# Delta rule's block inverses grown from 16 to 32 as 32x32 products on parts of the array, with a new plan for the order

## The chip, the cores and the metric

One core of a Trainium2 chip runs the program. The metric is the device time of one execution in microseconds (us). The kernel before has a median of 947.4 us over 3 runs (946.87 to 948.32).

## The reference, cut to what matters

Five layers follow each other on a sequence of 256 tokens with 1024 channels: a gated feed-forward layer (f1), a mixer of two attentions (mx), a second feed-forward layer (f2), a block attention (mb) and a gated delta rule (gd). The change bears on the delta rule, which solves a triangular system for each head and each chunk of 64 tokens:

```python
lmat = jnp.einsum('bhncd,bhnjd->bhncj', k_beta, k) * decay_strict
a_mat = lmat + jnp.eye(C, dtype=lmat.dtype)
rhs = jnp.concatenate([v * beta[..., None], k_beta * jnp.exp(g_cum)[..., None]], axis=-1)
sol = lax.linalg.triangular_solve(a_mat, rhs, left_side=True, lower=True, unit_diagonal=True)
```

There are 8 heads. The kernel takes two chunks together as one 128x128 triangle, two triangles a head, and inverts the triangles.

## The kernel before, in words

The whole program is recorded operation by operation, and a planner inside the kernel (`Program.schedule`) then writes the five engines' instruction streams in an order that it works out from ranks, readiness, free buffers and its own prices. So a change of one operation, or of a number in `PLAN`, can move instructions anywhere. Each engine executes its stream in that order. When TensorE's queue has nothing ready, the planner puts in filler matmuls (`bank<-ones 128x128`) whose results nobody reads. All instructions carry the line of one helper, L490, so the trace is read by engine, tile names and shapes. Tiles come from pools: `long` and `half` (fp32 in SBUF), `cut` (the two rounded parts of an fp32 operand, high and low, that ScalarE (ACT) and VectorE (DVE) write one after the other), `bank` (PSUM).

The start (`start`) loads x and c, takes SiLU of c, and builds the first layer's shift and scale from it chunk by chunk: for each of 8 chunks of 128 channels DVE makes weighted sums of the rows of `w_mod` (`long<-long,c_silu`), a one-column matmul turns them into the columns `A_f` and `B_f`, ACT makes the layer's input h from them (`half<-long,B_f,A_f`), and h and the two weight blocks of the chunk (`w_gate`, 1024 wide, and `w_up`, 768 wide) are cut into high and low parts. Then 42 matmuls of the chunk run. `PLAN["ahead"]` says from which chunk on the sums of the next chunk are recorded ahead of this chunk's weights.

The delta rule (`gdn`) has four units u of two heads, so four triangles a unit. `follow` records its steps in the order of `PLAN["gdn"]`: `k` (keys, which fill the triangles Lm), `s` (substitute: the inverses X of all 16x16 diagonal blocks, by DVE, gathered through DRAM into `xc`), `q`, `v`, `z` (projections), `g` (grow, in three parts), `r` (recur: the chain of products that gives the outputs of two heads, ending in a normalisation, a transposition and a cut) and `o` (the output projection, 512-wide matmuls). `grow` before spreads X and its transposed Xt out to block-diagonal 128x128 matrices, makes two rounds of four 128x128 products to get from blocks of 16 to blocks of 32, transposes Xt by TensorE to get X, and only from 32 on works on parts of the array: 32x32 products for 64, and 64x64 products for 128:

```python
for i in range(4):
    mm(ps[:, i, :], lm[:, i, :], Xt[u][:, i, :], start=True, stop=True)
z = self.half(4, P)
V.tensor_tensor(z, ps, self.up16[:, None, :].to_broadcast([P, 4, P]), ALU.mult)
```

Of the kernel before, what the change touches and what calls it, by code (L numbers as in the profile page):

```python
# [15 lines left out]
AF = mybir.ActivationFunctionType  # L16
ALU = mybir.AluOpType
AX = mybir.AxisListType

P = 128  # L20
# [105 lines left out]
class Program:  # L126
# [205 lines left out]
    def schedule(self):  # L332
        ops = self.ops
        for op in ops:
# [150 lines left out]
    def emit(self):  # L485
# [36 lines left out]
    "decay": 0,  # L522
}

# [30 lines left out]
class Net:  # L555
# [406 lines left out]
    def start(self):  # L962


        nc, a = self.nc, self.a
        for t in range(NT):
            nc.sync.dma_start(self.x[t], a["x"][0, t * P : (t + 1) * P, :])
        self.silu("c")
        view = a["w_mod"][0][:, 0 : 2 * D].rearrange("(p k) (s n) -> p k s n", k=KD, s=2)

        def partial(k0, nk):
# [25 lines left out]
        for t in range(NT):  # L997
# [16 lines left out]
        for n, (k0, nk) in enumerate(chunks):  # L1014
# [3 lines left out]
            ps = self.bank()  # L1018
# [12 lines left out]
            for k in range(k0, k0 + nk):  # L1031
# [461 lines left out]
    def gdn_consts(self):  # L1493
        nc = self.nc

        consts = self.half(4, P)
        self.triu, self.tril, self.bd16, self.up16 = (consts[:, i, :] for i in range(4))
# [5 lines left out]
        for m, n, sel in ((self.bd16, 16, (([[-16, 8], [0, 16]], 0, 1), ([[16, 8], [0, 16]], 15, -1))),  # L1503
                          (self.up16, 32, (([[-32, 4], [0, 32]], 0, 1), ([[32, 4], [0, 32]], 15, -1), ([[0, 4], [1, 32]], -16, 0)))):
            nc.gpsimd.tensor_copy(m, self.ones)
            v = m.rearrange("p (b j) -> p b j", j=n)
            for pattern, base, mul in sel:
                nc.gpsimd.affine_select(out=v, in_=v, pattern=pattern, compare_op=ALU.is_ge, fill=0.0, base=base, channel_multiplier=mul)
        self.al, self.dtb = (self.fixed_tile([P, 8], n) for n in ("al", "dtb"))
        for t, n in ((self.al, "gdn_a_log_2"), (self.dtb, "gdn_dt_bias_2")):  # L1510
            v = self.a[n][0]
            nc.sync.dma_start(t, bass.AP(tensor=v.tensor, offset=v.offset, ap=[[0, P], [1, 8]]))
        nc.scalar.activation(self.al, self.al, AF.Exp)
        yield

    def gdn(self, h, after, due):
        nc, a = self.nc, self.a
        V = nc.vector
        w_in = a["gdn_w_in_2"][0]
        tp, mm = nc.tensor.transpose, nc.tensor.matmul  # L1520
# [41 lines left out]
        ps = self.bank()  # L1562
# [16 lines left out]
        for u in range(4):  # L1579
# [6 lines left out]
            ps = self.bank(4, P)  # L1586
# [4 lines left out]
            exps = nc.used(ps)  # L1591
            ps = self.bank(4, P)
# [91 lines left out]
        def grow(u):  # L1684

            xc = blocks[0]
            both = self.long(2, 4, P)
            X, Xt[u] = both[:, 0], both[:, 1]
            lm = Lm[u].rearrange("p h t j -> p (h t) j")
            for n, dst in ((1, Xt[u]), (0, X)):  # L1690
                V.tensor_tensor(dst.rearrange("p i (b j) -> p i b j", b=8), xc[:, n, 4 * u : 4 * u + 4, None, :].to_broadcast([P, 4, 8, 16]),
                                self.bd16.rearrange("p (o b j) -> p o b j", o=1, b=8).to_broadcast([P, 4, 8, 16]), ALU.mult)
            ps = self.bank(4, P)
            for i in range(4):
                mm(ps[:, i, :], lm[:, i, :], Xt[u][:, i, :], start=True, stop=True)
            z = self.half(4, P)
            V.tensor_tensor(z, ps, self.up16[:, None, :].to_broadcast([P, 4, P]), ALU.mult)
            ps = self.bank(4, P)
            for i in range(4):
                mm(ps[:, i, :], X[:, i, :], z[:, i, :], start=True, stop=True)  # L1700
            V.tensor_tensor(Xt[u], Xt[u], ps, ALU.add)
            ps = self.bank(4, P)
            for i in range(4):
                tp(ps[:, i, :], Xt[u][:, i, :], self.ident)
            nc.scalar.activation(X, ps, AF.Copy)
            yield
            q = [slice(32 * j, 32 * j + 32) for j in range(4)]
            ps, z = self.bank(4, P), self.half(4, P)
            for lo, hi in ((0, 1), (2, 3)):
                for i in range(4):  # L1710
                    mm(ps[q[lo], i, 0:32], lm[q[hi], i, q[lo]], Xt[u][q[hi], i, q[hi]], start=True, stop=True)
                nc.scalar.activation(z[q[lo], :, 0:32], ps[q[lo], :, 0:32], AF.Copy)
            ps = self.bank(4, P)
            for lo, hi in ((0, 1), (2, 3)):
                for i in range(4):
                    mm(ps[q[lo], i, 0:32], X[q[lo], i, q[lo]], z[q[lo], i, 0:32], start=True, stop=True)
            for i in range(4):
                mm(ps[q[1], i, 0:32], z[q[0], i, 0:32], X[q[0], i, q[0]], start=True, stop=True)
            for lo, hi in ((0, 1), (2, 3)):
                nc.scalar.activation(Xt[u][q[lo], :, q[hi]], ps[q[lo], :, 0:32], AF.Copy)  # L1720
            nc.scalar.activation(X[q[1], :, q[0]], ps[q[1], :, 0:32], AF.Copy)
            yield
            lo, hi = slice(0, 64), slice(64, P)
            ps, z = self.bank(4, P), self.half(4, P)
            for i in range(4):
                mm(ps[lo, i, 0:64], lm[hi, i, lo], Xt[u][hi, i, hi], start=True, stop=True)
            nc.scalar.activation(z[lo, :, 0:64], ps[lo, :, 0:64], AF.Copy)
            ps = self.bank(4, P)
            for i in range(4):
                mm(ps[lo, i, 0:64], X[lo, i, lo], z[lo, i, 0:64], start=True, stop=True)  # L1730
            nc.scalar.activation(Xt[u][lo, :, hi], ps[lo, :, 0:64], AF.Copy)

        def recur(u, Xt, oT):
            hs = [2 * u, 2 * u + 1]
# [81 lines left out]
        Xt = [None] * 4  # L1816
# [122 lines left out]
```

## Time and profile before

| what | value |
|---|---|
| median of 3 runs | 947.4 us |
| the profiled execution | 948.18 us, its span 946.4 us |
| PE (TensorE) busy | 919.9 us, 97% of the span |
| DVE busy | 765.8 us, 81% |
| ACT busy | 520.4 us, 55% |
| mean granted TensorE clock | 0.992 |

PE stands for TensorE's matmuls, PEld for its weight loads, SP for the queue that issues the transfers. The records of matmuls overlap, each with the latency of one, so a PE that is "busy" throughout need not be fed at its best pace: the number of records in a stretch, and the distance between their starts, say more than the share.

### The profile page before, as it was taken

How to read it: one execution, taken by the hardware profiler on the slowest of the kernel's cores; microseconds unless marked ns; L12 is line 12 of the kernel's file. 1: busy time of each engine (PE TensorE's matmuls, PEld its weight loads, DVE VectorE, ACT ScalarE, POOL GpSimd, SP SyncE). 2: the span in 40 equal slices, each digit the busy share in tenths (PEclk: the TensorE clock that was granted, in tenths of full speed). 3: DMA queues.
4: the chain of work that ended last, by engine and by line, in shares of the span. 5: the costliest groups of instructions: out<-in, count | busy, mean ns of one | idle time of the engine just before them, and what ended most of it. 6: DMA issues, size and time to landing. Idle time of an engine off the chain costs nothing.

```text
span 946.4 us, 17955 instructions
## 1 busy us (share of the span) xinstructions
PE 919.9 (97%) x6925; PEld 855.4 (90%) x6925; DVE 765.8 (81%) x1401; ACT 520.4 (55%) x945; POOL 47.7 (5%) x98
## 2 busy tenths in 40 slices
PE   7999999998999999999999999999999989999996
PEld 7889999998999989988998999989999889999885
DVE  6995589968899989979998764579955699799566
ACT  5474533338862676558444544465565386655560
POOL 7000000002100000001000000000000000200010
PEclk7999999999999999999999999999999999999998
DMA  9997889983352749996999886628955531364101
GB/s 314 348 356 264 300 277 344 353 293 106 112 179 89 251 131 335 347 389 215 341 345 364 317 296 197 191 91 302 385 182 165 171 90 46 101 196 134 47 23 44
DMA packets 153969, 213.66 MB, mean 226 GB/s; under 512 B 14449, under 2 KB 127127, under 8 KB 153884
## 3 DMA queue, kind: packets, MB, share of 16 engines
q1 hardware_dynamic: 153884, 212.52, 66.1%
q8 instruction: 54, 0.88, 0.4%
q14 instruction: 31, 0.25, 0.1%
HBM read 210.11 MB, written 2.36 MB: 225 GB/s over the span
## 4 chain that ended last, share of the span: by engine, by line
PE 82%; DVE 9%; ACT 3%; DMA 3%; issue 2%; SPq 1%; POOL 1%; DVEq 0%; ACTq 0%; POOLq 0%
PE bank L490 82%; DVE half L490 3%; DVE long L490 2%; DVE cut L490 2%; DVE x L490 1%; SPq L490 1%; ACT junk L490 1%; ACT cut L490 1%; DMA long<-in_w_gate_dram 1%; DVE tiny L490 1%; ACT half L490 1%; POOL tiny L490 1%; DMA long<-in_w_up_dram 1%; DMA half<-in_g_pre_ffn_dram 0%; DMA long<-in_gdn_w_in_dram 0%
## 5 line engine op out<-in xcount | busy, mean ns | idle before, releaser
L490 PE MATMUL bank<-cut,cut 128*128 128x256 f32 (+2 forms) x5684 | 793.7, 299 | 4.7 <-DVE cut L490 3.1
L490 PEld LDWEIGHTS bank<-cut,cut 128*128 128x128 f32 x5684 | 735.4, 188 | 44.9 <-DVE cut L490 4.7
L490 DVE TENSOR_TENSOR cut<-long,cut 128x1024 fp32r<-128x1024 f32 (+3 forms) x290 | 341.7, 1194 | 80.5 <-PE bank L490 59.1
L490 ACT ACTIVATE cut<-long 128x1024 fp32r<-128x1024 f32 (+2 forms) x290 | 291.9, 1034 | 139.4 <-PE bank L490 102.6
L490 DVE SCALAR_TENSOR_TENSOR long<-long,c_silu,long 128x1024 f32<-128x1024 f32 (+1 forms) x144 | 142.9, 1013 | 1.0 <-DMA long<-in_w_mod_dram 0.2
L490 ACT ACTIVATE long<-bank 128x512 f32<-128x512 f32 (+9 forms) x148 | 62.6, 448 | 49.1 <-PE bank L490 46.6
L490 POOL TENSOR_TENSOR tiny<-tiny,mhalf 128x1 f32<-128x1 f32 (+1 forms) x32 | 30.9, 965 | 893.2 <-DVE tiny L490 893.2
L490 ACT ACTIVATE half<-bank 128x512 f32<-128x512 f32 (+4 forms) x75 | 35.3, 483 | 39.1 <-PE bank L490 38.8
L490 ACT ACTIVATE cut<-half 128x256 fp32r<-128x256 f32 (+3 forms) x70 | 32.9, 495 | 41.5 <-DVE half L490 41.0
L490 DVE TENSOR_TENSOR cut<-half,cut 128x256 fp32r<-128x256 f32 (+1 forms) x77 | 37.1, 512 | 10.0 <-ACT cut L490 10.0
L490 DVE SCALAR_TENSOR_TENSOR half<-bank,c_cols,half 128x253 f32<-128x253 f32 (+2 forms) x72 | 33.7, 477 | 2.1 <-ACT half L490 1.5
L490 DVE TENSOR_TENSOR half<-bank,long 128x512 f32<-128x512 f32 x20 | 13.7, 690 | 22.5 <-PE bank L490 22.4
L490 ACT ACTIVATE junk<-bank 128x128 bf16<-128x128 f32 (+1 forms) x44 | 16.0, 364 | 25.9 <-DVE half L490 21.7
L490 PE MATMUL bank<-half,long 128*128 128x128 f32 (+3 forms) x240 | 29.4, 258 | 0.0
L490 PE MATMUL bank<-ident,long 128*128 128x128 f32 (+1 forms) x162 | 24.8, 284 | 4.6 <-DVE long L490 3.6
L490 PE MATMUL bank<-long,long 128*128 128x128 f32 (+6 forms) x288 | 28.8, 282 | 0.3 <-ACT long L490 0.3
L490 PE MATMUL bank<-ident,half 128*128 128x128 f32 (+3 forms) x140 | 26.6, 276 | 1.8 <-DMA half<-in_g_pre_ffn_dram 0.9
L490 PEld LDWEIGHTS bank<-long,long 128*64 128x64 f32 (+4 forms) x288 | 20.9, 150 | 6.3 <-issue 1.3
L490 PEld LDWEIGHTS bank<-half,long 128*128 128x128 f32 (+2 forms) x240 | 24.6, 161 | 2.2 <-ACT half L490 0.6
L490 PEld LDWEIGHTS bank<-ident,long 128*128 128x128 f32 (+1 forms) x162 | 19.2, 144 | 6.9 <-DVE long L490 4.9
L490 DVE TENSOR_SCALAR tiny<-tiny 128x1 f32<-128x1 f32 (+3 forms) x67 | 11.6, 172 | 17.1 <-ACT junk L490 15.8
L490 ACT ACTIVATE half<-half,tiny 128x128 f32<-128x128 f32 (+2 forms) x36 | 16.7, 466 | 14.5 <-DVE tiny L490 14.5
(155 smaller groups left out, 509.3 us busy)
## 6 DMA issues: line engine op xcount, KB each, us to landing
long<-in_w_mod_dram SPq DMA_DIRECT2D x56, 512.0 KB, 4.6
long<-in_ada_w_dram SPq DMA_DIRECT2D x48, 512.0 KB, 6.9
long<-in_w_gate_dram SPq DMA_DIRECT2D x44, 512.0 KB, 7.7
long<-in_w_down_dram SPq DMA_DIRECT2D x44, 512.0 KB, 8.9
long<-in_w_up_dram SPq DMA_DIRECT2D x38, 512.0 KB, 7.2
long<-in_w_in_dram SPq DMA_DIRECT2D x38, 512.0 KB, 4.7
long<-in_moba_w_in_dram SPq DMA_DIRECT2D x32, 512.0 KB, 4.6
long<-in_gdn_w_in_dram SPq DMA_DIRECT2D x24, 512.0 KB, 4.0
```

What stands on the lines that cost most here:

```text
L490: getattr(engine, method)(*[real(a) for a in args], **{k: real(v) for k, v in kw.items()})
```

## The change

`grow` no longer spreads the 16x16 blocks out first. It keeps them as 32 columns a triangle (`d`, with X and Xt side by side), and makes the two rounds from 16 to 32 as 32x32 products, four parts of the array in turn: 16 products a unit, then 32, of which 16 give X directly, so that the transposition falls away. After that d is spread out to `Xt[u]` (128 columns) and to half of `X`, off to the side of the next 32x32 products, which read d itself. Two small DVE reductions and three POOL instructions make the masks. In the start, c is loaded and its SiLU taken ahead of x, and `ahead` falls from 9 to 4. `raw` copies the first gate projections of the delta rule and takes their SiLU after the exponentials, `exps` lets the SiLUs of keys and queries go between them. Two steps change places in the mixer, `v0` goes behind the grows, k2 ahead of k1, and two background tasks change places.

```diff
-        self.window, self.counted, self.slow, self.table, self.array = 0.0, 0.0, 2, "exp", (P, P)
+        self.window, self.counted, self.slow, self.table, self.array = 0.0, 0.0, 2, "silu", (P, P)
...
-    "f2": (7, 4, 9, 4, 4, 8, 0, 0, 0, 0, 0),
+    "f2": (8, 3, 9, 4, 4, 8, 0, 0, 0, 0, 0),
     "mixer": (
-        "a v i p . . x0 d2 d1 x1 d0 . s d3 d4 d5 . d6 h0 d7 u5 h1 u0 d8 h2 . h3 . . . e0 . "
-        ". e0 . u3 e1 . u2 e1 . u4 . . u1 . . . u7 z3 z0 . u6 . . z1 . . . . . . z2 ."
+        "a v i p . . x0 d2 d1 x1 d0 . s d3 d4 d5 . d6 h2 h0 d7 . u5 h1 u0 d8 . h3 . . e1 e0 "
+        ". e0 . u3 . u2 . e1 . u4 . . u1 . . . u7 z3 z0 u6 . . . z1 . . . . . z2 . ."
     ),
...
-    "gdn": "k0 k1 k2 k3 s0 q0 q1 g3 g0 q2 q3 g0 z2 g3 g2 z1 g3 g0 v0 g1 g1 g2 g1 r0 v2 v1 r1 g2 o0 r2 . v3 r3",
+    "gdn": "k0 k2 k1 k3 s0 q0 q1 g3 g0 q2 q3 g0 z2 g3 g2 z1 g3 g0 g1 g1 g2 g1 v0 r0 v2 v1 r1 g2 o0 r2 . v3 r3",
...
-    "background": (0, 1, 9, 2, 3, 5, 4, 6, 7, 10, 8),
+    "background": (0, 1, 9, 3, 2, 5, 4, 6, 7, 10, 8),
...
-    "ahead": 9,
+    "ahead": 4,
...
-    "raw": False,
-    "exps": True,
+    "raw": True,
+    "exps": False,
...
+        self.silu("c")
         for t in range(NT):
             nc.sync.dma_start(self.x[t], a["x"][0, t * P : (t + 1) * P, :])
-        self.silu("c")
...
-            both = self.long(2, 4, P)
-            X, Xt[u] = both[:, 0], both[:, 1]
...
+            all = self.long(1024)
+            d, X = all[:, 0:256].rearrange("p (n i j) -> p n i j", n=2, i=4), all[:, 512:768].rearrange("p (i j) -> p i j", i=4)
+            for n in (1, 0):
+                V.tensor_tensor(d[:, n].rearrange("p i (b j) -> p i b j", b=2), xc[:, n, 4 * u : 4 * u + 4, None, :].to_broadcast([P, 4, 2, 16]),
+                                self.bd16.rearrange("p (o b j) -> p o b j", o=1, b=2).to_broadcast([P, 4, 2, 16]), ALU.mult)
+            ps, z = self.bank(4, 32), all[:, 256:384].rearrange("p (i j) -> p i j", i=4)
+            with nc.side_by_side(3):
+                for i in range(4):
+                    for s in q:
+                        mm(ps[s, i, :], lm[s, i, s], d[s, 1, i, :], start=True, stop=True)
+            V.tensor_tensor(z, ps, self.up16[:, None, :].to_broadcast([P, 4, 32]), ALU.mult)
+            ps = self.bank(2, 4, 32)
+            with nc.side_by_side(3):
+                for i in range(4):
+                    for s in q:
+                        mm(ps[s, 1, i, :], d[s, 0, i, :], z[s, i, :], start=True, stop=True)
+                for i in range(4):
+                    for s in q:
+                        mm(ps[s, 0, i, :], z[s, i, :], d[s, 0, i, :], start=True, stop=True)
+            V.tensor_tensor(d, d, ps, ALU.add)
```

On TensorE, the place in the delta rule behind the last 256-wide projection, where the grows begin. Before (the names after the arrow are the moving operand and the weights; `x4` are four products in a row):

```order
4959 L490 MATMUL bank_166<-long_101,long_90 128x128 x4
4960 L490 MATMUL bank_163<-long_96,long_86 128x128 x4
4961 L490 MATMUL bank_165<-long_98,long_91 128x128 x3
4962 L490 MATMUL bank_168<-half_107,long_101 128x128 x4
4963 L490 MATMUL bank_169<-half_108,long_96 128x128 x4
4964 L490 MATMUL bank_165<-long_98,long_91 128x128
4965 L490 MATMUL bank_166<-ident,long_101 128x128 x4
4966 L490 MATMUL bank_163<-long_101,long_90 32x32 x4
4967 L490 MATMUL bank_168<-long_93,long_87 128x128
4968 L490 MATMUL bank_162<-ident,long_96 128x128 x4
```

The same place now:

```order
4961 L490 MATMUL bank_163<-long_100,long_97 32x32 x16
4962 L490 MATMUL bank_168<-long_90,long_103 32x32 x16
4963 L490 MATMUL bank_169<-long_101,long_88 32x32 x16
4964 L490 MATMUL bank_164<-long_93,long_92 32x32 x16
4965 L490 MATMUL bank_168<-ones 128x128
4966 L490 MATMUL bank_169<-ones 128x128
4967 L490 MATMUL bank_164<-ones 128x128 x2
4968 L490 MATMUL bank_163<-long_100 32x32 x32
4969 L490 MATMUL bank_168<-long_90 32x32 x32
4970 L490 MATMUL bank_169<-long_101 32x32 x32
4971 L490 MATMUL bank_164<-long_100,long_97 32x32 x8
4972 L490 MATMUL bank_163<-long_93 32x32 x32
```

The 128x128 products and the transpositions (`ident`) of the grows are gone, 48 products of 32x32 a unit stand in their place, and all four units now begin at once. By the two orders whole, TensorE loses 32 products and 16 transpositions of 128x128, has 272 products of 32x32 instead of 80, 32 of 64x64 as before, and 38 fillers instead of 34.

On ACT, the head of the program, where the SiLU of c is taken. Before:

```order
1 L490 ACT_TABLE_LOAD
2 L490 ACTIVATE junk,tiny_114<-x_171 128x512 x2
3 L490 ACTIVATE junk,tiny_116<-x_172 128x512 x2
4 L490 ACT_TABLE_LOAD
5 L490 ACTIVATE c_silu<-c_raw 128x8
6 L490 ACTIVATE long_95<-bank_162 128x4x128
```

Now:

```order
1 L490 ACT_TABLE_LOAD
2 L490 ACTIVATE c_silu<-c_raw 128x8
3 L490 ACTIVATE junk,tiny_114<-x_171 128x512 x2
4 L490 ACTIVATE junk,tiny_116<-x_172 128x512 x2
5 L490 ACTIVATE long_95<-bank_162 128x4x128
```

The SiLU stands ahead of the squares of x, and one table load is gone.

On DVE, the end of the start: the cuts of the last weights, the last columns `A_f` and the low half of the last chunk of h (`cut<-half`). Before:

```order
86 L490 TENSOR_TENSOR cut_80<-long_91,cut_74 128x1024
87 L490 TENSOR_TENSOR long_93<-long_93 128x256
88 L490 TENSOR_TENSOR cut_79<-long_90,cut_76 128x768
89 L490 SCALAR_TENSOR_TENSOR A_f_179<-bank_167,c_cols 128x1
90 L490 TENSOR_TENSOR B_f_180<-bank_167,c_cols 128x1
91 L490 SCALAR_TENSOR_TENSOR A_f_179<-A_f_179,c_cols 128x1
92 L490 TENSOR_TENSOR cut_84<-long_95,cut_82 128x1024
93 L490 TENSOR_TENSOR cut_63<-long_98,cut_81 128x1024
94 L490 TENSOR_TENSOR cut_85<-long_103,cut_83 128x1024
95 L490 TENSOR_TENSOR cut_77<-half_111,cut_77 128x2x128
```

Now:

```order
85 L490 TENSOR_TENSOR long_90<-long_90 128x256
86 L490 TENSOR_TENSOR cut_76<-long_88,cut_72 128x768
87 L490 SCALAR_TENSOR_TENSOR A_f_179<-bank_167,c_cols 128x1
88 L490 TENSOR_TENSOR B_f_180<-bank_167,c_cols 128x1
89 L490 SCALAR_TENSOR_TENSOR A_f_179<-A_f_179,c_cols 128x1
90 L490 TENSOR_TENSOR cut_80<-long_93,cut_75 128x1024
91 L490 TENSOR_TENSOR cut_79<-long_99,cut_74 128x768
92 L490 TENSOR_TENSOR cut_81<-long_94,cut_82 128x1024
93 L490 TENSOR_TENSOR cut_66<-long_103,cut_85 128x1024
94 L490 TENSOR_REDUCE half_110<-half_112 128x32
95 L490 COPY c_cols<-bank_167 128x77
96 L490 TENSOR_TENSOR cut_73<-half_108,cut_73 128x2x128
```

The last columns are made ahead of the last chunk's two weight cuts instead of behind them, and two other cuts instead of three stand ahead of the low half of h. On ACT the high half of that h now stands behind three cuts, before behind one.

## Rows read from the trace of the kernel before

**Rows 1.** The page, part 1: busy us (share of the span) x instructions.

```profile
PE 919.9 (97%) x6925; PEld 855.4 (90%) x6925; DVE 765.8 (81%) x1401; ACT 520.4 (55%) x945; POOL 47.7 (5%) x98
```

**Rows 2.** Windows: stretch and its length, busy us of each engine (x instructions), clock, DMA.

```profile
core 0: us, PE busy (x) PEld busy (x) DVE busy (x) ACT busy (x) POOL busy (x), PEclk, DMA share, GB/s
...
25.00:63.00 38.00, 34.82 (x280) 33.11 (x278) 37.98 (x92) 21.07 (x30) 0.00 (x0) 1.00 1.05 346
...
218.00:230.00 12.00, 9.54 (x70) 8.49 (x69) 11.03 (x21) 11.54 (x25) 2.69 (x2) 1.00 0.40 122
230.00:430.00 200.00, 199.56 (x1588) 184.93 (x1587) 178.98 (x424) 124.44 (x247) 5.31 (x6) 1.00 0.66 227
...
753.00:771.00 18.00, 14.94 (x101) 13.01 (x100) 17.63 (x36) 10.81 (x22) 1.94 (x2) 1.00 0.20 59
...
857.00:874.20 17.20, 17.20 (x148) 17.06 (x147) 16.11 (x31) 9.79 (x20) 1.01 (x1) 1.00 0.62 172
874.20:907.90 33.70, 33.32 (x397) 29.32 (x396) 19.69 (x42) 19.50 (x58) 1.01 (x1) 1.00 0.15 48
```

**Rows 3.** Timeline of PE from the first grow on: start, duration, engine, operation, records.

```profile
874.24 2.62 PE L490 MATMUL bank<-long,long 128*128 128x128 f32 x22
...
878.71 0.60 PE L490 MATMUL bank<-ident,long 128*128 128x128 f32 x4
879.24 0.85 PE L490 MATMUL bank<-long,long 32*32 32x32 f32 x10
...
887.23 1.14 PE L490 MATMUL bank<-half,long 64*64 64x64 f32 x16
...
907.97 0.94 PE L490 MATMUL bank<-cut,cut 128*128 128x512 f32 x3
908.74 1.72 PE L490 MATMUL bank<-half,long 128*128 128x128 f32 x14
...
923.11 14.82 PE L490 MATMUL bank<-cut,cut 128*128 128x512 f32 x63
```

**Rows 4.** Timeline of PE, 892.9 to 893.7 us: 32x32 products of three kinds.

```profile
893.07 0.34 PE L490 MATMUL bank<-long,long 32*32 32x32 f32 x5
893.22 0.21 PE L490 MATMUL bank<-half,long 32*32 32x32 f32 x1
893.25 0.19 PE L490 MATMUL bank<-long,long 32*32 32x32 f32 x1
...
893.31 0.19 PE L490 MATMUL bank<-half,long 32*32 32x32 f32 x1
893.31 0.19 PE L490 MATMUL bank<-long,long 32*32 32x32 f32 x1
893.31 0.21 PE L490 MATMUL bank<-long,half 32*32 32x32 f32 x1
...
893.43 0.32 PE L490 MATMUL bank<-long,half 32*32 32x32 f32 x5
```

**Rows 5.** Timeline of PE, 882.7 to 884.5 us: 32x32 products into one bank.

```profile
882.75 0.35 PE L490 MATMUL bank<-half,long 32*32 32x32 f32 x7
882.91 0.21 PE L490 MATMUL bank<-long,half 32*32 32x32 f32 x1
...
882.97 0.19 PE L490 MATMUL bank<-long,half 32*32 32x32 f32 x1
882.97 0.19 PE L490 MATMUL bank<-half,long 32*32 32x32 f32 x1
```

**Rows 6.** Timelines of DVE and ACT in the delta rule: a grow's spreading, a recur's first copy.

```profile
863.58 2.49 DVE L490 TENSOR_TENSOR long<-half,half 128x512 f32<-128x512 f32 x4
...
890.34 0.39 ACT L490 ACTIVATE half<-bank 128x256 f32<-128x256 f32 x1 [0.43 <-PE bank L490]
```

**Rows 7.** Timelines of ACT, DVE and PE in the start.

```profile
7.49 1.28 ACT L490 ACT_TABLE_LOAD   x1
...
9.62 1.71 DVE L490 TENSOR_SCALAR long<-long,c_silu 128x256 f32<-128x256 f32 x2
...
59.14 3.50 DVE L490 TENSOR_TENSOR cut<-long,cut 128x1024 fp32r<-128x1024 f32 x3
62.55 0.42 DVE L490 TENSOR_TENSOR cut<-half,cut 128x256 fp32r<-128x256 f32 x1
...
63.02 17.14 PE L490 MATMUL bank<-cut,cut 128*128 128x256 f32 x117 [1.07 <-DVE cut L490]
```

**Rows 8.** Windows of PE alone in the start.

```profile
10.00:12.00 2.00, 1.69 (x8) 0.50 1.06 364
18.00:20.00 2.00, 2.00 (x11) 0.57 1.25 305
```

More of the change, by code (lines that the diff above doesn't have):

```diff
@@ L1496, in gdn_consts @@
         consts = self.half(4, P)
-        self.triu, self.tril, self.bd16, self.up16 = (consts[:, i, :] for i in range(4))
+        self.triu, self.tril, self.bd32 = (consts[:, i, :] for i in range(3))
+        self.bd16, self.up16 = consts[:, 3, 0:32], consts[:, 3, 32:64]
         for m, step, base in ((self.triu, 1, 0), (self.tril, -1, -1)):
@@ L1500, in gdn_consts @@
             nc.gpsimd.affine_select(out=m, in_=m, pattern=[[step, P]], compare_op=ALU.is_ge, fill=0.0, base=base, channel_multiplier=-step)
-        for m, n, sel in ((self.bd16, 16, (([[-16, 8], [0, 16]], 0, 1), ([[16, 8], [0, 16]], 15, -1))),
-                          (self.up16, 32, (([[-32, 4], [0, 32]], 0, 1), ([[32, 4], [0, 32]], 15, -1), ([[0, 4], [1, 32]], -16, 0)))):
+        wide = self.half(2, P)
+        for m, dst, n, sel in ((self.bd32, None, 32, (([[-32, 4], [0, 32]], 0, 1), ([[32, 4], [0, 32]], 31, -1))),
+                               (wide[:, 0], self.bd16, 16, (([[-16, 8], [0, 16]], 0, 1), ([[16, 8], [0, 16]], 15, -1))),
+                               (wide[:, 1], self.up16, 32, (([[-32, 4], [0, 32]], 0, 1), ([[32, 4], [0, 32]], 15, -1), ([[0, 4], [1, 32]], -16, 0)))):
             nc.gpsimd.tensor_copy(m, self.ones)
@@ L1508, in gdn_consts @@
                 nc.gpsimd.affine_select(out=v, in_=v, pattern=pattern, compare_op=ALU.is_ge, fill=0.0, base=base, channel_multiplier=mul)
+            if dst is not None:
+                nc.vector.tensor_reduce(dst, m.rearrange("p (b j) -> p j b", j=32), AX.X, ALU.add)
         self.al, self.dtb = (self.fixed_tile([P, 8], n) for n in ("al", "dtb"))
@@ L1686, in grow @@
             xc = blocks[0]
-            both = self.long(2, 4, P)
-            X, Xt[u] = both[:, 0], both[:, 1]
             lm = Lm[u].rearrange("p h t j -> p (h t) j")
[L1690 to L1704, printed above, removed]
@@ L1705, in grow @@
-            nc.scalar.activation(X, ps, AF.Copy)
+            q = [slice(32 * j, 32 * j + 32) for j in range(4)]
+            lo, hi = slice(0, 64), slice(64, P)
+            all = self.long(1024)
[3 more added lines that the diff above has]
+                                self.bd16.rearrange("p (o b j) -> p o b j", o=1, b=2).to_broadcast([P, 4, 2, 16]), ALU.mult)
@@ new lines, in grow @@
+            V.tensor_tensor(d, d, ps, ALU.add)
+            ps, z = self.bank(4, 32), all[:, 384:512].rearrange("p (i j) -> p i j", i=4)
+            with nc.side_by_side(2):
+                for i in range(4):
+                    for a, b in ((0, 1), (2, 3)):
+                        mm(ps[q[a], i, :], lm[q[b], i, q[a]], d[q[b], 1, i, :], start=True, stop=True)
+            for a in (0, 2):
+                nc.scalar.activation(z[q[a]], ps[q[a]], AF.Copy)
+            Xt[u] = Xts[u]
+            for n, dst, s in ((1, Xt[u], slice(0, P)), (0, X[lo], lo)):
+                m, k = s.stop, dst.shape[2] // 32
+                V.tensor_tensor(dst.rearrange("p i (b j) -> p i b j", j=32), d[s, n, :, None, :].to_broadcast([m, 4, k, 32]),
+                                self.bd32[s, 0 : 32 * k].rearrange("p (o b j) -> p o b j", o=1, j=32).to_broadcast([m, 4, k, 32]), ALU.mult)
@@ L1706, in grow @@
             yield
-            q = [slice(32 * j, 32 * j + 32) for j in range(4)]
-            ps, z = self.bank(4, P), self.half(4, P)
-            for lo, hi in ((0, 1), (2, 3)):
+            ps = self.bank(2, 4, 32)
+            with nc.side_by_side(2):
                 for i in range(4):
-                    mm(ps[q[lo], i, 0:32], lm[q[hi], i, q[lo]], Xt[u][q[hi], i, q[hi]], start=True, stop=True)
-                nc.scalar.activation(z[q[lo], :, 0:32], ps[q[lo], :, 0:32], AF.Copy)
-            ps = self.bank(4, P)
@@ L1714, in grow @@
-            for lo, hi in ((0, 1), (2, 3)):
+                    for a in (0, 2):
+                        mm(ps[q[a], 1, i, :], d[q[a], 0, i, :], z[q[a], i, :], start=True, stop=True)
                 for i in range(4):
[L1716 to L1720, printed above, removed]
@@ L1721, in grow @@
-            nc.scalar.activation(X[q[1], :, q[0]], ps[q[1], :, 0:32], AF.Copy)
-            yield
[L1723 to L1730, printed above, removed]
@@ L1731, in grow @@
-            nc.scalar.activation(Xt[u][lo, :, hi], ps[lo, :, 0:64], AF.Copy)
+                    mm(ps[q[1], 0, i, :], z[q[0], i, :], d[q[0], 0, i, :], start=True, stop=True)
+            for a, b in ((0, 1), (2, 3)):
+                nc.scalar.activation(Xt[u][q[a], :, q[b]], ps[q[a], 1], AF.Copy)
+            nc.scalar.activation(X[q[1], :, q[0]], ps[q[1], 0], AF.Copy)
+            yield
+            ps, z = self.bank(4, 64), all[:, 768:1024].rearrange("p (i j) -> p i j", i=4)
+            with nc.group():
+                for i in range(4):
+                    mm(ps[lo, i, :], lm[hi, i, lo], Xt[u][hi, i, hi], start=True, stop=True)
@@ L1733, in recur @@
+            nc.scalar.activation(z[lo], ps[lo], AF.Copy)
+            ps = self.bank(4, 64)
+            with nc.group():
+                for i in range(4):
+                    mm(ps[lo, i, :], X[lo, i, :], z[lo, i, :], start=True, stop=True)
+            nc.scalar.activation(Xt[u][lo, :, hi], ps[lo], AF.Copy)
         def recur(u, Xt, oT):
@@ L1815, in gdn @@
         steps = dict(k=keys, q=queries, v=values, z=lambda u: u < PLAN["firsts"][2] - 1 or z_proj(u), s=lambda u: substitute(), g=grow, r=lambda u: recur(u, Xt[u], oT), o=output)
-        Xt = [None] * 4
+        Xt, Xts = [None] * 4, self.pairs(4, 4, P)
         going = self.follow("gdn", steps)
```

## The prediction

> **What bounds the kernel now.** I read the page first: TensorE is busy for 97% of the span, DVE for 81% [rows 1]. Records of matmuls overlap with their latency, so I went through windows and compared what a stretch holds (records by the distance of their starts) with its length. In most of the program both agree: of the 200 us from 230 on PE is busy for 199.56 us, and DVE, at 178.98, keeps up [rows 2]. There only less work for PE helps. Three kinds of stretch differ. In the start, DVE is busy for 37.98 of 38 us and the DMA share is 1.05, while PE has 34.82 [rows 2]: DVE and the transfers set the pace together. At three change-overs between layers PE lacks some 3 us each (2.5 and 3.1 in the two that end at 230 and 771), while DVE or ACT is full [rows 2]. The third is the tail, from the first grow on.
>
> The tail is bound by latencies. At 874.24 the last projection is through and the grows begin; at 890.34 ACT makes the first recur's copy, 16.1 us later [rows 3, 6]; the first 512-wide product of the output projection starts at 907.97, 17.6 us behind the copy; the last ends at 923.11 + 14.82 = 937.9 [rows 3]. From the first grow that is 63.7 us. PE looks full in 874.2 to 907.9 (33.32 of 33.7 us), and yet starts only 397 records there, many of them some 20 ns apart, with DVE at 19.69 and ACT at 19.50 [rows 2, 4]. From the counts and distances I get 24.8 us of useful work, 1.3 of fillers and some 7.6 in which PE waits for copies. So fewer rounds, or cheaper ones, before the first recur shorten this stretch; the same inverses do not come out earlier because DVE is fast: the spreading ran at 863.58, 10.7 us ahead of the first grow [rows 6].
>
> **The change, part by part.** *The prices of the products.* A 128x128 product of fp32 has two records: x14 in 1.72 us with the last one's latency of some 0.2 in it is 0.108 us a record, 0.215 a product [rows 3]. Transpositions: the four that start at 878.71 are through when the next starts at 879.24 [rows 3]: 0.11 each. The sixteen 64x64 records in 1.14 us give about 0.06, 0.13 a product [rows 3]. A filler costs as much as a product, 0.21.
>
> The price of the new 32x32 products, four parts of the array in turn, is the open one, since grow before uses at most two parts at once. Alone, one part starts five records from 893.07 to 893.22, 30 ns a record; seven from 882.75 to 882.91, 23 ns [rows 4, 5]. Where products of two units and of two parts mix, thirteen start between 893.22 and 893.43, 16 to 17 ns a record [rows 4]. Bounds: at the top no overlap at all, 23 to 30 ns; at the bottom a quarter of that for four parts, about 7 ns. I take 17, the nearest row to a mixed stream.
>
> The Trainium skill ("TensorE: Matmul & The Clock Gate", Part 3) has tiles of different rows of the array start about 4 ns apart, which would put four of them near the lower bound; by that the tail would gain about 2.5 us more than below.
>
> *The tail now.* By the order, 272 products of 32x32, 16 of the 64x64 ones and 12 fillers stand ahead of the first recur's first product. 272 x 2 x 17 ns = 9.2 us; 16 x 0.13 = 2.1; 12 x 0.21 = 2.6; about ten changes between shapes at 0.09 us (878.71 to 879.24 is 0.53 us, less 4 x 0.11 [rows 3]) = 0.9. Together 14.8 us, and with the last copy of ACT the first recur starts about 15.6 behind the first grow, against 16.1. Recur is untouched; its chain from copy to output keeps 17.6 us: 33.2. Behind the first output stood 96 products of 512 at 0.23 us (x63 in 14.82 [rows 3]) = 22.2, 22 of 128x128 = 4.7 and 12 transpositions = 1.3: 28.2 of the 30.0 us. Now, by the order, 15 of the 128x128 products remain there: 26.7. Of the 1.8 us of waiting I leave 0.5, since twelve 512-wide products now stand right ahead of the last four transpositions, more than the stall of half a microsecond that the copies cause there. 33.2 + 27.2 = 60.4 against 63.7: **-3.3 us**. At 7 ns a record the products cost 5.4 us less, of which I count half, since waits for DVE and ACT then show: -5.8. At 23 to 30 ns it is 0 to +3.8; the break-even lies near 25 ns a record.
>
> *The start.* c's SiLU leads and one table load of 1.28 us goes from ACT's head [rows 7]; the first sums, which need it, start at 9.62 on DVE [rows 7] and may come by that earlier. At the end of the start, three cuts of 3.50 us together stand ahead of the low half of the last h, and PE, which needs it, waits 1.07 us for it and starts at 63.02 [rows 7]; now two cuts stand there, about 1.1 us less. But ACT's high half now stands behind three cuts instead of one, and the transfers, full at 1.05 [rows 2], do not get faster. From 0 (transfers decide) to -2.1; I take **-0.8**.
>
> *Change-overs.* Three fillers fewer by the order, at most 0.2 us each, and order changes where DVE or ACT is full: **-0.4**, from +0.5 to -1.
>
> *At nothing:* the mixer's exchanged steps, f2's pace, the two background tasks and v0 behind the grows stand in PE's full stretches [rows 2], where order moves no end. `raw` and `exps` change ACT's table loads ahead of the grows, DVE's spreads of 256 instead of 512 are shorter, and the masks' extra POOL and DVE work lies far ahead (POOL is at 5% [rows 1]). The cover of all these is the 10.7 us by which the spread blocks wait for PE [rows 6]; without it a table load costs 1.28 us.
>
> Sum: -3.3 - 0.8 - 0.4 = -4.5 us. The profiled execution takes 948.2 us (span 946.4 and 1.8 around it), 0.8 above the median; 947.4 - 4.5 gives **943.0 us**.
>
> **Rivals.** *One part at a time.* The four parts of a round write to one bank of PSUM, and each could wait for the other's write. Then a record costs 23 to 30 ns [rows 4, 5], and with 0 to +3.8 in the tail and -1.2 elsewhere the time is 946 to 950. Against it: two products of different parts have the same start, 882.97 [rows 5], and by the order they write to the same bank. The Trainium skill ("TensorEngine Tiling (Array Packing)", Restrictions and Gotchas) says that different row tiles cannot access the same bank at once; it would give this rival's time, and the row disagrees with it as far as starts tell. 15%.
>
> *Each change of the part costs like a change of shape* (slower). 192 products more, each on another part than the one before, at 0.09 us as between 128x128 and 32x32 [rows 3], are +17 us, and the time about 957. It decides from some 0.025 us a change on. Against it speak the starts 10 to 30 ns apart where parts alternate [rows 4]. 7%.
>
> *The clock.* In the start PE is granted 0.50 at 10 to 12 us and 0.57 at 18 to 20, with 8 and 11 records in 2 us [rows 8]. The tail now has a stretch of some 15 us of small products. If the clock fell there for 9 us, as in the start, half of it would be lost, 4.5 us, which eats the gain: about 947. Against it: before, with 397 records in 33.7 us, it was granted 1.00 [rows 2]. 7%.
>
> *More.* Four parts at 7 ns a record, or the start at its lower bound of -2.1: 937 to 940. 9%.
>
> **How the numbers follow.** The forecast (940 to 945.5) has 62%. Above it lie the serial parts and the clock, at 945.5 to 950 (22%), and the 957; below it the 9%. A range of 938 to 947 leaves out the 957, most of the serial case and the deepest part of the gains, together 2 in 10. What the measurement tells from no change is about 0.2%, 1.9 us: faster ends at 945.5, slower begins at 949.3. Faster: 62 + 9 and 1 of the clock, 72%. The same: the clock's other 6, and 9 of the serial parts, 15%. Slower: 13%, of the serial parts 6 and the costly change of parts 7.
>
> **What will show it.** In the timeline of PE from the first grow on: 32x32 records 17 ns apart (7: more; 25 or above: the serial rival). First grow to the first recur's copy: 15.6 us; copy to the first 512-wide output: 17.6; from there to the last end: 27.2. The granted clock in the tail: 1.00. The start of PE's long stretch at 63.02 comes 0.8 earlier, and the first sums at 9.62 by up to 1.3. I would be wrong if the rounds turn out bound by DVE's and ACT's copies between them, which then show as PE idle with no gain from cheap products, or if the first grow comes late behind the spread.

## The result and the profile after

The changed kernel takes 956.1 us (median of 4 runs, 955.3 to 956.7) against 947.9 in the same runs of the kernel before: 1.0089 times as long, 95% interval 1.0076 to 1.0102. The forecast was 943.0, faster than before; the kernel came out 8.3 us slower. The profiled execution has a span of 954.9 us, 8.5 more than before.

Page of the changed kernel, part 1, to set against [rows 1]:

```profile
PE 926.1 (97%) x7237; PEld 861.1 (90%) x7237; DVE 763.4 (80%) x1411; ACT 517.1 (54%) x944; POOL 47.0 (5%) x101
```

The share of PE says nothing of the loss; the waits of PE do (idle time by releaser: sum, times, longest):

```profile
PE bank L490 <- issue: 4.2, 2, 2.1
```

"issue" is idle time for which the profile shows no releaser; the kernel before has no such row. Windows of the changed kernel, columns as in [rows 2]:

```profile
218.00:230.00 12.00, 9.49 (x70) 8.48 (x69) 11.11 (x21) 11.54 (x25) 2.69 (x2) 1.00 0.36 111
753.00:771.00 18.00, 14.96 (x99) 12.97 (x98) 17.17 (x34) 10.01 (x21) 1.95 (x2) 1.00 0.11 30
874.50:877.90 3.40, 3.40 (x213) 3.04 (x213) 2.78 (x11) 0.78 (x3) 0.00 (x0) 1.00 0.80 242
877.90:880.00 2.10, 0.01 (x2) 0.01 (x2) 1.68 (x4) 0.81 (x1) 0.00 (x0) 1.00 0.08 31
880.00:881.40 1.40, 1.35 (x128) 1.25 (x128) 0.59 (x2) 0.00 (x0) 0.00 (x0) 1.00 0.05 12
881.40:883.40 2.00, 0.00 (x0) 0.00 (x0) 2.00 (x5) 0.00 (x0) 0.00 (x0) 0.60 0.00 0
883.40:890.00 6.60, 6.56 (x167) 5.79 (x168) 4.80 (x11) 3.21 (x12) 0.00 (x0) 0.50 0.02 5
890.00:912.00 22.00, 22.00 (x172) 19.70 (x173) 3.94 (x8) 10.56 (x29) 0.00 (x0) 0.50 0.30 96
912.00:918.00 6.00, 6.00 (x49) 5.73 (x49) 4.37 (x15) 3.92 (x15) 1.01 (x1) 0.96 0.01 3
```

The change-overs lack as much of PE as before. The tail differs: TensorE stands still for 2.1 us, executes 128 matmul records (two to an fp32 product) and 128 weight loads in 1.4 us, stands still for 2 us again, and from then on is granted half its clock until about 912.5. The same place in the timeline of PE:

```profile
874.55 1.44 PE L490 MATMUL bank<-long,long 32*32 32x32 f32 x128
875.94 1.17 PE L490 MATMUL bank<-ones 128*128 128x128 f32 x8
877.04 0.85 PE L490 MATMUL bank<-long 32*32 32x32 f32 x76
879.99 1.17 PE L490 MATMUL bank<-long 32*32 32x32 f32 x114 [2.09 <-issue]
...
883.44 0.26 PE L490 MATMUL bank<-long,long 32*32 32x32 f32 x2 [2.09 <-issue]
```

The first 128 records in 1.44 us, the last one's latency of some 0.2 in it, are 10 ns a record with four parts of the array: nearer the lower bound of 7 than the 17 that I took. Both idle stretches lie within a row of products that one copy had already released, so no round waits there. Between them lie just 256 instructions, 128 records and 128 loads. The DMA view of 880 to 882 has one packet of the queue of instructions:

```profile
q8 instruction: 1, 0.02, 3.2%
```

In windows of 0.2 us such packets stand at 877.6, 881.0 and 884.4, 3.4 us apart, and each stop ends some 2.4 us behind its packet (879.99, 883.44). The pages count 54 such packets in the program before and 57 now, for 2 x 6925 and 2 x 7237 matmul records and loads of TensorE: a packet for every 254 to 256 of them. So TensorE uses a packet's 256 instructions up in 1.4 us here and waits for the next.

The landmarks of the tail: the first recur's copy on ACT, then the first and the last stretch of 512-wide products on PE.

```profile
898.53 0.38 ACT L490 ACTIVATE half<-bank 128x256 f32<-128x256 f32 x1
```

```profile
918.45 1.71 PE L490 MATMUL bank<-cut,cut 128*128 128x512 f32 x6 [0.17 <-ACT cut L490]
...
933.71 12.74 PE L490 MATMUL bank<-cut,cut 128*128 128x512 f32 x54
```

From the first grow at 874.55: 24.0 us to the copy (forecast 15.6), 19.9 to the first output (17.6), 28.0 to the end at 946.45 (27.2); 71.9 in sum, against 63.7 before and 60.4 forecast.

### The profile page after: what moved, and what is told of

Same layout as the page of the kernel before. It is cut to its first block, busy times and chain, and to the rows that moved or that the text cites. A ratio compares the mean times of both kernels' runs of the same rounds, so it can differ in the third digit from the quotient of the medians.

```text
span 954.9 us, 18597 instructions
## 1 busy us (share of the span) xinstructions
PE 926.1 (97%) x7237; PEld 861.1 (90%) x7237; DVE 763.4 (80%) x1411; ACT 517.1 (54%) x944; POOL 47.0 (5%) x101
## 5 line engine op out<-in xcount | busy, mean ns | idle before, releaser
L490 ACT ACTIVATE cut<-long 128x1024 fp32r<-128x1024 f32 (+3 forms) x290 | 292.1, 1034 | 147.8 <-PE bank L490 110.5
L490 ACT ACTIVATE long<-bank 128x512 f32<-128x512 f32 (+9 forms) x156 | 63.7, 432 | 61.0 <-PE bank L490 57.8
L490 POOL TENSOR_TENSOR tiny<-tiny,mhalf 128x1 f32<-128x1 f32 (+1 forms) x32 | 29.3, 915 | 902.5 <-DVE tiny L490 895.6
L490 ACT ACTIVATE half<-bank 128x512 f32<-128x512 f32 (+2 forms) x63 | 32.0, 519 | 36.7 <-PE bank L490 36.5
L490 DVE SCALAR_TENSOR_TENSOR half<-bank,c_cols,half 128x255 f32<-128x255 f32 (+2 forms) x72 | 33.3, 477 | 2.7 <-ACT half L490 2.0
L490 PE MATMUL bank<-long,long 32*32 32x32 f32 (+6 forms) x384 | 28.2, 271 | 2.1 <-issue 2.1
L490 PE MATMUL bank<-long 32*32 32x32 f32 (+5 forms) x512 | 27.1, 244 | 2.5 <-issue 2.1
L490 PEld LDWEIGHTS bank<-long,long 32*32 32x32 f32 (+4 forms) x384 | 21.4, 150 | 7.5 <-issue 3.6
L490 PEld LDWEIGHTS bank<-long 32*32 32x32 f32 (+4 forms) x512 | 22.6, 146 | 4.4 <-issue 2.9
L490 ACT ACTIVATE half<-half,tiny 128x128 f32<-128x128 f32 (+2 forms) x36 | 16.7, 465 | 13.7 <-DVE tiny L490 13.7
L490 DVE TENSOR_SCALAR tiny<-tiny 128x1 f32<-128x1 f32 (+3 forms) x67 | 11.3, 171 | 14.6 <-ACT junk L490 13.1
```

The costliest lines, as they stand in the source:

```text
L490: getattr(engine, method)(*[real(a) for a in args], **{k: real(v) for k, v in kw.items()})
```

## The experiments

There are two theories for the idle stretches, **code** (TensorE runs out of instructions, as above) and **rounds** (it waits for copies between the rounds), and two for the clock, **idle** (it falls because TensorE stands still) against **small** (it falls because small products use little of the array). Times are medians, each beside runs of the kernel before on the same chip (947.4 to 947.6).

**Is it code?** `twice` changes the emission of the changed kernel:

```diff
-            for method, args, kw in op.calls:
+            twice = op.engine == "tensor" and op.parts == (32, 32) and len(op.calls) >= 16
+            for method, args, kw in op.calls * (2 if twice else 1):
```

> The changed kernel with the 32x32 products of grow's first two rounds issued twice (192 products, so 384 weight loads and 384 products more as instructions), the same results. Code: TensorE uses up a 16 KB block of its instructions (256 of them) in 1.4 us there, and blocks come 3.4 us apart; three blocks more give about three more idle stretches of 2 us with no releaser, five in all, and 7 to 11 us more than the changed kernel. Rounds: if the two idle stretches are waits for copies between the rounds, their number stays at two, and the added products cost what such products cost, 20 ns at full clock or 46 at half: 4 to 9 us.

It takes 968.2 us (965.9 to 968.7), 12 more than the changed kernel. The waits of PE:

```profile
PE bank L491 <- issue: 8.9, 5, 2.7
```

Five idle stretches instead of two, three for three blocks more, as code has it and rounds doesn't. The time is a little above code's 7 to 11.

`wide_fill` puts in wide fillers (`small` is an op of 12 or more 32x32 products):

```diff
...
+                if small and i and i % 12 == 0:
+                    bank = args[0].t.slot[:, 256:512]
+                    self.nc.tensor.matmul(bank.rearrange("p (b j) -> p b j", b=2), ones, ones[:, None, :].to_broadcast([P, 2, P]), start=True, stop=True)
```

> The changed kernel with a filler of 256 columns (0.43 us at full clock) behind every 12 of the 32x32 products within a round, into free columns of the same bank; 16 of them, about 6.9 us. Code: the fillers stretch 256 instructions from 1.4 to 3 us and more, blocks arrive in time, the idle stretches of 2.09 us shrink below 0.8 us in sum, the clock stays at 1.00, and the time is 946 to 950 in spite of the work added. Rounds: the idle stretches stay, and the time is the changed kernel's plus up to 7 us, 956 to 963.

It takes 950.4 us over 10 runs (948.9 to 960.5), 1.0047 (1.0021 to 1.0072) times before: less than the changed kernel, with more work. The trace has 12 of these fillers, not the 16 of the expectation; by the starts in the timeline (874.86 to 875.49 for the first) each takes 0.63 us with its changes of shape, 7.6 us in all. In the profiled execution (949.6) no idle time is without releaser, and the clock holds (windows of PE: busy, clock, DMA, GB/s):

```profile
874.00:880.00 6.00, 6.00 (x168) 1.00 0.56 172
880.00:885.00 5.00, 5.00 (x170) 1.00 0.01 3
885.00:890.00 5.00, 5.00 (x173) 1.00 0.01 3
890.00:900.00 10.00, 9.61 (x175) 1.00 0.31 107
```

Two of its runs (956.8 and 960.5) have a mean clock of 0.987 and 0.982, where the others have 0.990 to 0.997; there the clock seems to have fallen after all, but they have no trace. The landmarks of the profiled one:

```profile
897.79 0.38 ACT L495 ACTIVATE half<-bank 128x256 f32<-128x256 f32 x1
```

```profile
911.48 1.70 PE L495 MATMUL bank<-cut,cut 128*128 128x512 f32 x6
...
926.73 12.74 PE L495 MATMUL bank<-cut,cut 128*128 128x512 f32 x54
```

From its first grow at 874.54 these are 23.3, 13.7 and 28.0 us. The order of its own products is that of the changed kernel, and none of the added fillers stands behind 888. So the stretch from the copy to the first output prices the clock: 13.7 us at 1.00, 19.9 in the changed kernel, which has half the clock up to 912.5. That is 6.2 us, more than the 4.2 of the two stops. Less 7.6 of fillers, the 64.9 us of its tail are 57.3, and the stretch ahead of the copy is 15.7, as forecast. This estimate leaves out waits that the fillers may hide. By it the changed kernel's 71.9 us are 14.6 too long, of which 4.2 are the stops and some 10 the clock.

**What lets the clock fall?** `part_fill` narrows the fillers to one part:

```diff
...
-                    bank = args[0].t.slot[:, 256:512]
+                    bank, part = args[0].t.slot[0:32, 256:512], ones[0:32]
```

> As the kernel with wide fillers, but each filler uses one 32x32 part of the array only (256 columns through 32 rows and 32 columns of weights), so that TensorE's time is filled with the same number of instructions and columns while 15 of 16 parts rest. The blocks of code come in time again if the fillers stretch them (idle with no releaser below 1 us in sum). Small: if small products don't keep the clock up, it falls to 0.50 all the same within the grows, and the time is 956 to 963. Idle: if what let the clock fall is that TensorE stood still, it stays at 1.00, and the time is that of the wide fillers, 949 to 951.

It takes 955.5 us (953.7 to 956.4). Idle without releaser is down to 1.4 us in two pieces (0.8 the longest), and still:

```profile
885.00:888.00 3.00, 2.43 (x68) 1.00 0.00 0
888.00:890.00 2.00, 2.00 (x68) 0.84 0.03 8
890.00:900.00 10.00, 10.00 (x97) 0.50 0.34 107
```

The clock falls with a TensorE that stands still for 1.4 us in sum: small products don't keep it up, as "small" has it, though the stops were not quite gone (1 us was the condition) and the time is just below the 956 that "small" gave. `hold` and `hold_long` make TensorE of the kernel before wait where the grows begin:

```diff
...
+            if op in held:
+                bank = op.calls[0][1][0].t.slot
+                self.nc.tensor.matmul(bank[:, :P], ones, ones, start=True, stop=True)
+                for _ in range(3):
+                    self.nc.scalar.activation(self.junk.real(), bank[:, :], AF.Copy)
```

> The kernel before, with TensorE held up twice for about 2.2 us where the grows begin (ahead of the first and the third unit's first round, it waits for three copies of ACT out of a bank), all its own products as they were. Idle: standing still there is what lets the clock fall; it goes to 0.50 within a few us and stays for 10 us or more, and the time is 956 to 962 (4.4 of waiting, 5 to 10 of half clock). Small: if the clock of the changed kernel falls because small products don't keep it up, it stays at 1.00 here, and the time rises by the waits alone, at most 4.4 us: 949 to 952.

> The kernel before with the two holds made longer, seven copies of ACT each instead of three, about 4.2 us each. Idle: if enough standing still lets the clock fall whatever the products are, it goes to 0.50 here, and the time is 960 or more (8.4 of waiting, and 5 to 10 of half clock, less 2 that the tail's other waits take up). Small: it stays at 1.00, and the time is 954 to 957.

`hold` takes 953.6 us (951.9 to 955.0), between its two forecasts. In the profiled execution (952.3) there are two waits of 2.0 us, and the clock stays at 1.00:

```profile
874.00:880.00 6.00, 2.27 (x18) 1.00 0.00 0
```

`hold_long` takes 961.5 us (961.2 to 961.6), as "idle" had it. It has two waits of 4.5 us, and the clock falls towards the end of the first, with products of the whole array alone around it:

```profile
874.00:878.00 4.00, 0.21 (x2) 1.00 0.05 22
878.00:880.00 2.00, 1.33 (x6) 0.51 0.00 0
...
895.00:900.00 5.00, 4.74 (x79) 1.00 0.63 196
```

So neither theory is right alone. Standing still for 4.5 us does it, twice 2.0 us didn't in the execution that was profiled, and small products do it with little standing still. The burst of the changed kernel has both, and which of them its fall needs is not shown.

**Which part of the change?** `old_grow` is the kernel before with the changed plan and start, `new_grow` the kernel before with the new grow alone.

> The changed kernel with grow and its masks as before: the new plan and start alone. If what the change loses lies in the new grow (TensorE stands still for 2.09 us twice there, then 30 us at half clock), this kernel has neither and takes what the first grow's start says, 0.3 us more than before: 947 to 949. If the new plan itself costs the 8 us, it takes 953 or more.

> The kernel before with the new grow and its masks alone; plan, start, raw and exps as before. Grow: if the new grow costs what the change loses, its burst of small products is here too: one or more idle stretches of 2 us with no releaser, a fall of the clock, and 953 to 960. Plan: if the new plan and the grow don't suit each other, it takes 943 to 950.

Both times miss. `old_grow` takes 952.8 us (951.0 to 956.0), between its two forecasts: the new plan with the old grow loses 5.4 us. In its profiled execution, the fastest (951.0), it is level with before at 761.87, and then TensorE waits 1.56 us for DVE ahead of the grows, the first of which starts at 876.01 instead of 874.24. The tail from there is 63.5 us, before's 63.7, and the rest of the program's end takes 1.3 more. Where the other executions lose up to 5 us more is open. `new_grow` takes 960.3 us (951.8 to 961.5), just above its first forecast, with two idle stretches without releaser (2.4 us in all) and half the clock from about 875 to 902.5. One of its four runs, 951.8 with a mean clock of 0.994 against 0.976 to 0.980 of the others, seems to have kept the clock. So the fall comes with the new grow under either plan, if not in every execution; and the two losses, 5.4 and 12.8, don't add up to the 8.3 of both together.

**Can it be mended?** `t_first` gathers the transposed inverses first, `dve_t` lets DVE make X:

```diff
-            for n, src in enumerate((xb, xbt)):
+            for n, src in ((1, xbt), (0, xb)):
```

```diff
...
-                for i in range(4):
-                    for s in q:
-                        mm(ps[s, 0, i, :], z[s, i, :], d[s, 0, i, :], start=True, stop=True)
-            V.tensor_tensor(d, d, ps, ALU.add)
+            V.tensor_tensor(d[:, 1], d[:, 1], ps, ALU.add)
+            V.transpose(d[:, 0], d[:, 1])
```

> The changed kernel with the transposed inverses gathered through DRAM ahead of the plain ones. The first round needs only the transposed ones, and in the trace of the changed kernel they are gathered second and spread at 874.21, just ahead of the first grow. Now 64 of the 272 products run up to 9 us earlier between the projections. Code: the burst then has 256 instructions fewer, so one idle stretch at most of 2.1 us, or none; if the clock stays at 1.00, 944 to 950; if the clock falls all the same, 952 to 956.

> The changed kernel with X at 32 taken from X's transposed by DVE, which transposes 32x32 blocks within themselves (one instruction a unit), instead of by 16 products of TensorE a unit: 64 products, so one block of 256 instructions, less within the grows. Code: one idle stretch of 2 us with no releaser goes; if the clock stays up with it, the time falls to 946 to 949, if the clock falls all the same, to 951 to 955. Rounds: if DVE's copies between the rounds were the limit, a transposition more on DVE makes it slower than the changed kernel, above 956.

`t_first` takes 958.2 us (957.3 to 961.4), `dve_t` 959.3 (954.8 to 960.4). Each has one idle stretch of 2.0 us instead of two, as code has it, but the clock falls in both, at about 879 and 882. One block less is not enough. Both times lie above what code gave (952 to 956 and 951 to 955). That of `dve_t`, above 956, is what rounds gave: from 870 on its trace has 2.2 us of waits for DVE's `long`, which the changed kernel lacks there, 1.4 of them before and in the grows. So a part of its loss is DVE's; only the fastest of its runs has a trace, and what the others lost is open.

The next six tell the planner of the code (`BLOCK` is 3450 ns). They also have a new order of the delta rule's steps and new ranks, found with that rule; all but two of them (`dve_t_told`, `dve_t_fill`) have `ahead` at 5, and `told_b` and `both_c` have `raw` off. No run has the rule without a new order.

```diff
...
+        self.code += sum(2 if m == "transpose" or args[1].dtype == F32R else 4 for m, args, _ in op.calls)
+        if self.code >= 256:
+            self.code -= 256
+            now = self.block = max(now, self.block + self.BLOCK)
```

> The changed kernel with the planner told of the code: in its prices of TensorE a block of 256 instructions can't begin less than 3.45 us after the one before, and for that rule it has a new order of the delta rule's steps (ranks of g and r, ahead 5). The products are the same. Code: the idle stretches without releaser shrink, since other units' rounds and fillers stand between the small products; if the clock then stays at 1.00, 944 to 948. If the small products hold the clock down even so, 952 to 957.

> Both together: X at 32 by DVE's transposition, and an order from the planner that is told of the code. Code: no idle stretch without releaser over 1 us; with the clock at 1.00 it takes 940 to 944 and beats both kernels; with a fall of the clock in the grows 948 to 953.

> As the kernel with both, with a filler of 256 columns behind every 12 products of the first two rounds: 8 of them, 3.4 us of TensorE's time. Small: if the small products let the clock fall in the kernel without them, this one keeps it at 1.00 and is the faster of the two, 942 to 946; if that one keeps its clock, this one is 2 to 3 us slower than it.

The orders of these three leave work out: in `told` one unit's inverses are taken from an unfinished triangle, and in all three unit 2's recur runs without its growth from 64 to 128, whose products still run. `told` takes 951.9 us (948.7 to 958.3), `dve_t_told` 941.5 (940.6 to 945.2), `dve_t_fill` 946.2 (945.6 to 950.8). `told` still has a stop of 2.1 us, and half the clock behind it. In `dve_t_told` the only wait without releaser is 0.3 us, and its clock is 1.00 from 874 to 930; the eight fillers, which it doesn't need, cost 4.7 us instead of 2 to 3. Since work was missing, three more have orders that keep everything; that of `told_b`:

```diff
...
-    "gdn": "k0 k2 k1 k3 s0 q0 q1 g3 g0 q2 q3 g0 z2 g3 g2 z1 g3 g0 g1 g1 g2 g1 v0 r0 v2 v1 r1 g2 o0 r2 . v3 r3",
+    "gdn": "k0 k2 k1 k3 s0 q0 q1 g3 g0 q2 q3 g0 z2 g3 z1 g2 g3 g0 g1 g2 g1 g1 v0 r0 v2 v1 r1 g2 o0 r2 . v3 r3",
```

> The changed kernel, every product of it, with the planner told of the code (no block of 256 instructions of TensorE begins less than 3.45 us after the one before) and an order of the delta rule's steps that suits that rule and keeps every step behind what it reads. Code: one idle stretch of 2 us at most; with the clock at 1.00, 944 to 948; with a fall of the clock 949 to 957. In either case faster than the changed kernel.

> X at 32 by DVE's transposition of 32x32 blocks, and a planner told of the code, with an order that keeps every step behind what it reads. If a burst of fewer small products, with other work between its parts, is supplied with code and keeps the clock, no idle stretch without releaser is over 1 us, the clock is 1.00 in the tail, and the time is 940 to 945, faster than the kernel before. If the shorter time of the kernel that had this first came from the growth that it left out, 946 or more.

> As both_b, another order of the same steps (with the first gates' SiLU taken early, raw off). The same: 940 to 945 if code and clock are the cause; 946 or more if one lucky order was. If it has an idle stretch of 2 us or a fall of the clock and both_b has none, the one with them is 3 us or more slower.

`told_b` takes 945.7 us (945.1 to 947.2 in 10 runs), 0.9983 (0.9974 to 0.9992) times before, with the changed kernel's own products. `both_c` takes 943.6 us (942.3 to 950.0), 0.9964 (0.9949 to 0.9980), the fastest complete one by its median. `both_b` takes 945.8 us, 0.9977 (0.9954 to 1.0000), above its forecast of 940 to 945, but in two groups: five runs at 941.0 to 943.7 with a mean clock of 0.993 to 0.997, five at 947.8 to 948.8 with 0.985 to 0.989. The profiled executions of both have no idle time without releaser in the tail and a clock of 1.00 from 874 to 915. That of `both_b` is of its first group; that the clock falls in the others is read from the mean alone.

In the timeline of `told_b` fillers and a transposition stand between rounds of two units, and no idle stretch is without releaser:

```profile
875.52 0.75 PE L497 MATMUL bank<-long,long 32*32 32x32 f32 x64 [1.58 <-DVE long L497]
876.20 1.51 PE L497 MATMUL bank<-ones 128*128 128x128 f32 x8
877.64 1.93 PE L497 MATMUL bank<-long 32*32 32x32 f32 x128
879.50 1.86 PE L497 MATMUL bank<-ones 128*128 128x128 f32 x10
881.29 0.69 PE L497 MATMUL bank<-long,long 32*32 32x32 f32 x32
```

Even here the clock falls, behind the wait for DVE and with small products, but it is back within some 4 us (busy, clock, DMA, GB/s):

```profile
876.00:878.00 2.00, 2.00 (x66) 0.73 0.83 307
878.00:880.00 2.00, 2.00 (x122) 0.50 0.08 27
880.00:882.00 2.00, 2.00 (x43) 0.91 0.03 8
```

Its first recur's copy comes 17.0 us after the first grow (892.52), the first output 13.9 later (906.37), and the end at 935.5, 29.1 behind that: 60.0 us for the tail, where the forecast said 60.4.

## Why the prediction was wrong

- **The step that failed** is the price of the products ahead of the first recur, "272 x 2 x 17 ns = 9.2 us", as all that the burst costs. The pace of a product was better than that, 10 ns a record. But the sum has no term for the code: at a block of 256 instructions every 3.4 us and four instructions a product, a long burst comes to some 53 ns a product (an estimate from the packets). In the trace this is 4.2 us of standing still.
- **The clock** was a rival with 7% and a price of 4.5 us for 9 us at half clock. It came, and stayed for some 30 us (about 882 to 912.5); why so long is not shown. From the copy to the first output alone it cost 6.2 us against `wide_fill`, more than the two stops together, and by the estimate there some 10 us in the whole tail. "Against it: before, with 397 records in 33.7 us, it was granted 1.00" was a bad reason: 224 of the 397 were products on parts, but the other 173, of the whole array at 0.108 us, stood between them and took 18.7 us. In `part_fill` 32x32 products, with fillers on one part between them, did not hold the clock.
- **The tail** took 71.9 us, not 60.4. `told_b` has the same products, code in time and the clock down for only some 4 us, and takes 60.0 us. That this meets the forecast is in part luck: its parts are off in both directions (17.0, 13.9 and 29.1 for 15.6, 17.6 and 27.2). The 17.6 "keeps" of the copy to the output was too long at full clock (13.7 in `wide_fill`). That cheaper rounds shorten the tail was right; without code and clock in the sum it could not be had.
- **Serial parts and costly changes of part** did not come: 10 ns a record with four parts in turn is neither 23 to 30 nor a change of 90.
- **The start** was right: DVE's first sums begin at 8.35 instead of 9.62, and PE's long stretch at 61.97 instead of 63.02 [rows 7], 1.05 us earlier for the 0.8 forecast.
- **The change-overs** gave nothing: the third one's long stretch starts 0.45 us later than before (762.32 against 761.87) and the first grow 0.3 later, so the 1.05 was lost again before 762; at the first one 0.55 of it is left (229.68 against 230.23). Other executions of the same plan differ at the third by 0.5 (761.78 in `twice`), so where it went is open.
- **Two prices** of the prediction don't follow from its own terms: half of 5.4 us beyond -3.3 is -6.0, not -5.8, and 17 us on 943 is 960, not 957, unless what each product is priced at already is taken off first. Neither moved the forecast.
- **The cover of 10.7 us** was misread. The spreading at 863.58 [rows 6] is one of two, that of the plain inverses, which are gathered first; DVE of the kernel before spreads the transposed ones, which the first round needs, only here, and the first grow starts at 874.24:

```profile
873.22 2.49 DVE L490 TENSOR_TENSOR long<-half,half 128x512 f32<-128x512 f32 x4
```

In the changed kernel it cost nothing that the landmarks show, but `told_b` waits 1.58 us for it.

The Trainium skill ("Runtime: NRT & Kernel Launch", Instruction fetch mechanics) has the instructions come in blocks of 256, fetched ahead and for the most part hidden. The trace agrees with the block (128 matmul records and 128 loads between two stops), and disagrees with the hiding for this burst, by 2.09 us twice.

## What to carry to other kernels

Price a burst of small products by its instructions as well as by its columns: many tiny products in a row can wait for their own code. What helped here was other work between them (`told_b`), with part of them on another engine besides (`both_c`); fewer of them alone did not (`t_first`, `dve_t`). Such a stretch can cost more behind it than in it, if the clock falls in it and stays down: 4.2 us of stops here, 6.2 in the recur that follows. To price a lower clock, look for a run with the same products in the same order at the full one. And before a cover is claimed, check which of several like-named steps is the last one that the consumer needs.

## What the runs showed of the hardware

- Four parts of the array in turn start the records of 32x32 products 10 ns apart (128 records in 1.44 us).
- TensorE's code came in packets of some 256 instructions (54, 57 and 60 packets for 13850, 14474 and 15242 instructions in the kernel before, the changed one and `twice`). TensorE stood still when it had used one up before the next came (packets 3.4 us apart): 2.09 us twice here, up to 2.7 in `twice`.
- The granted clock fell to 0.50 in one wait of 4.5 us, not in two of 2.0 us (one profiled execution each), and it fell behind a stretch of 32x32 products with 1.4 us of idle time without releaser. With wide fillers of equal number and columns it stayed at 1.00 in the profiled execution.
- The same products in the same order took 13.7 us at full clock (`wide_fill`) and 19.9 at half for all but the last 6 us (the changed kernel), from the first recur's copy to the first output.
